# Where the normed rows are scaled: by row before the transposes or by column after them, in a three-block fp32 kernel

## The chip, the cores and the metric

One core of one Trainium2 chip. The metric is the time of one execution in microseconds (us) on the device, the median of several runs. TensorE (PE) has a granted clock that the profile shows as PEclk, 1.00 for full speed.

## The reference, cut to what matters

All tensors are fp32; 256 tokens, 1024 features, one batch. A vector `c` modulates the first two layers, and a memory of 256 rows feeds a cross-attention.

```python
c_act = silu(c)                                   # c / (1 + exp(-c)), 1024 numbers
for l in range(2):
    sh_m, sc_m, g_m, sh_f, sc_f, g_f = split(c_act @ ada_w[l] + ada_b[l], 6)
    h = modulate(rmsnorm(x, norm_g[l, 0]), sh_m, sc_m)      # h * (1 + scale) + shift, per feature
    if l == 0:  y = short_conv_mixer(h, ...)
    else:       # kv: its own shift, scale from c_act @ kv_ada_w + kv_ada_b and its own norm of the same x
                y = mla_mixer(h, ..., shared_kv(x, c_act, ...))
    x = x + g_m * rmsnorm(y, norm_g[l, 1])
    h = modulate(rmsnorm(x, norm_g[l, 2]), sh_f, sc_f)
    x = x + g_f * rmsnorm(relu(h @ mlp_up[l]) ** 2 @ mlp_down[l], norm_g[l, 3])
h = rms_norm(x, norm_mix);    x = x + concat(hgrn2(h @ w_in), moba(h @ w_in)) @ w_out
h = rms_norm(x, norm_xattn);  x = x + cross_attention(h, rms_norm(mem, norm_mem), w_q, w_k, w_v, w_o)
h = rms_norm(x, norm_mlp);    x = x + relu(h @ w_ff1) ** 2 @ w_ff2
return rms_norm(x, norm_final)
```

## The kernel before, in words

**Stages.** In this order: K and V of the memory (lines 553 to 618), the first norm (L620), conv mixer, MLP0, MLA (kv and q projections, attention, output), MLP1, HGRN and MoBA, cross-attention, MLP2, final norm. The residual x stays on chip as two token tiles `xt[tt]` of 128 tokens by 1024 features, each in halves `hf` of 512. Matmuls want features on the partitions, so each normed tile is transposed, 128x128 at a time, on PE.

**Three-term products.** Every fp32 operand is kept as a rounded part and the rest, and a product is three matmuls (`mm3`, `mm3t`, L237 to L246). `split_into` makes the parts: the high one on ScalarE (ACT, L220), the low one on VectorE (DVE, L221). Weights come by `load` (SP's DMA queue, into one of 7 raw buffers) and `split`.

**Order of work.** The program is written stage by stage, and each engine's order is then set by a scheduler from priorities (the order written; `tc.high_priority()` puts a block ahead of what waits beside it) and free buffers. Each engine then runs its own list in that order. `behind(marks, f)` issues what f issues after the marked instructions (the last high and low part that a norm wrote).

**Modulation.** `c_act @ ada_w` is done on DVE, one column of 128 outputs at a time: `ada_part`'s step loads 512 KB and multiplies it with `cb`, silu(c) on all partitions (L306, 112 steps). `background()`, called at each split, runs a planned number of such steps. `row(g)` turns 8 columns of 128 into a 1024-wide row on all partitions: two copies (gb), eight PE transposes (L326), two ACT copies. A norm before a modulated stage takes two rows, `norm_rows`: gain and shift. `to_features` then does, per half of a token tile:

```python
nc.vector.scalar_tensor_tensor(v, xt[tt][:, hf, :], r, a[:, c], op0=OP.mult, op1=OP.mult)   # L407
nc.vector.tensor_add(v, v, sh[:, c])                                                        # L409
nc.tensor.transpose(m[:, j * P:(j + 1) * P], v[:, j * P:(j + 1) * P], ident)                # L412, four
hi = activation(m, Copy); lo = m - hi                                                       # L398, L399
```

This happens at the first norm (L620 to L623), into MLP0 (m0, after conv_out), into MLA (two norms of one x: kv and q, `into_mla`), and into MLP1 (m1). The norms of the second half of the program have a gain row from DRAM and no shift.

**The opening.** `cb` is a DMA of c to all partitions, then exp, add, reciprocal and product on 128x1024 (L291 to L297). The memory's tiles are scaled by column and split (L560, L561); the K product (L237 to L239) starts with them; 16 modulation steps run beside it and x's first norm stands after the V product.

**Ends of projections.** `down` accumulates in four banks, acc[tt][hf]; its last 6 weight pieces (TAIL) are done for tt=0 first and tt=1 after, so that tt=0's norm runs beside tt=1's matmuls. `Mlp.rest` does the same. `Mlp.first`/`squares` make MLP pieces: relu, transposes, a copy (rT), square and split.

## Time and profile before

| | |
|---|---|
| Runs | 1062.53 us median of 3 (1059.4 to 1064.05) |
| Profiled execution | 1059.84 us; span 1058.0 us; mean granted PE clock 0.981 |
| Busy share of the span | PE 96% (1012.3 us, 6186 instructions), DVE 73% (768.3 us), ACT 52% (547.2 us), POOL 0% |
| DMA | 231.58 MB, mean 219 GB/s |
| Chain of work that ended last | PE 84%, DVE 8%, ACT 4%, issue 2%, DMA 1% |

The chain is followed back from the last instruction through whatever released each step, so its shares add up to the span. The busy shares are means over stages with different limits: PE fills most of the span, and what is left for any change to take is either PE work itself or the places where PE stands or runs below its full clock.

### The profile page before, as it was taken

The numbers are of one execution on the slowest core, as the hardware profiler recorded it, in microseconds if no ns is written. First come the engines' busy times: TensorE is split into PE (matmuls) and PEld (weight loads), VectorE is DVE, ScalarE is ACT, GpSimd is POOL, SyncE is SP. The second block draws the span as 40 slices with busy tenths as digits, with TensorE's granted clock in tenths as the row PEclk, the third lists the DMA queues.
The fourth block names the chain that finished last, engine by engine and source line by source line (L and its number), as shares of the span: only waits on it lengthen the run. The fifth ranks groups of instructions, "written<-read, shape, count | busy, mean of one in ns | idle before, by whom it ended". The sixth has DMA issues, their size and how long they took to land.

```text
span 1058.0 us, 16057 instructions
## 1 busy us (share of the span) xinstructions
PE 1012.3 (96%) x6186; PEld 882.9 (83%) x6186; DVE 768.3 (73%) x1140; ACT 547.2 (52%) x872; POOL 1.0 (0%) x8
## 2 busy tenths in 40 slices
PE   4989999999999979999999999999899999999997
PEld 4869997898898768677999888898678988998885
DVE  7889998998888699759765554778567557555552
ACT  5344456654345564768444444754246446544441
POOL 0000000000000000000000000000000000000000
PEclk9999999999999989999999999999799999999999
DMA  7979996899998369616876663755214426666511
GB/s 282 354 265 359 322 327 230 289 374 347 318 346 312 105 208 371 218 41 228 302 236 194 196 182 118 263 193 179 73 48 155 145 101 236 183 189 188 185 55 40
DMA packets 64876, 231.58 MB, mean 219 GB/s; under 512 B 7201, under 2 KB 7585, under 8 KB 64801
## 3 DMA queue, kind: packets, MB, share of 16 engines
q1 hardware_dynamic: 64512, 229.93, 63.2%
q8 instruction: 48, 0.79, 0.3%
q10 hardware_dynamic: 288, 0.65, 0.2%
q14 instruction: 28, 0.22, 0.1%
HBM read 229.50 MB, written 1.05 MB: 218 GB/s over the span
## 4 chain that ended last, share of the span: by engine, by line
PE 84%; DVE 8%; ACT 4%; issue 2%; DMA 1%; DVEq 0%; SPq 0%; ACTq 0%
PE u L238 11%; PE acc L246 11%; PE acc L244 11%; PE u L237 11%; PE u L239 11%; PE acc L245 11%; PE u L245 4%; PE u L246 4%; PE u L244 4%; PE m L249 3%; DVE wlo L221 2%; PE acc L249 1%; DVE raw L306 1%; ACT whi L220 1%; DMA raw<-in_w_xk_dram 1%
## 5 line engine op out<-in xcount | busy, mean ns | idle before, releaser
L221 DVE TENSOR_TENSOR wlo<-raw,whi 128x1024 fp32r<-128x1024 f32 (+1 forms) x317 | 380.1, 1212 | 138.9 <-ACT whi L220 135.9
L220 ACT ACTIVATE whi<-raw 128x1024 fp32r<-128x1024 f32 (+1 forms) x317 | 328.0, 1049 | 250.2 <-PE u L238 100.6
L238 PE MATMUL u<-hl,whi 128*128 128x256 f32 x960 | 271.2, 283 | 0.0
L239 PE MATMUL u<-hh,wlo 128*128 128x256 f32 x960 | 270.5, 282 | 0.0
L237 PE MATMUL u<-hh,whi 128*128 128x256 f32 x960 | 270.3, 282 | 0.0
L238 PEld LDWEIGHTS u<-hl,whi 128*128 128x128 f32 x960 | 181.3, 189 | 3.6 <-issue 2.5
L237 PEld LDWEIGHTS u<-hh,whi 128*128 128x128 f32 x960 | 181.8, 190 | 1.1 <-ACT hh L398 0.2
L239 PEld LDWEIGHTS u<-hh,wlo 128*128 128x128 f32 x960 | 181.5, 189 | 0.0
L244 PE MATMUL acc<-whi,mh 128*128 128x512 f32 x384 | 151.8, 395 | 0.0
L246 PE MATMUL acc<-wlo,mh 128*128 128x512 f32 x384 | 151.6, 395 | 0.0
L245 PE MATMUL acc<-whi,ml 128*128 128x512 f32 x384 | 151.4, 394 | 0.0
L306 DVE SCALAR_TENSOR_TENSOR raw<-raw,cb 128x1024 f32<-128x1024 f32 x112 | 135.7, 1219 | 11.0 <-DMA raw<-in_adaT_dram 11.0
L246 PEld LDWEIGHTS acc<-wlo,mh 128*128 128x128 f32 x384 | 72.2, 188 | 16.8
L245 PEld LDWEIGHTS acc<-whi,ml 128*128 128x128 f32 x384 | 72.2, 188 | 16.0
L244 PEld LDWEIGHTS acc<-whi,mh 128*128 128x128 f32 x384 | 72.1, 188 | 15.7
L245 PE MATMUL u<-whi,hl 128*128 128x512 f32 x144 | 57.9, 402 | 1.0 <-DVE hl L399 1.0
L244 PE MATMUL u<-whi,hh 128*128 128x512 f32 x144 | 57.1, 396 | 0.5 <-ACT hh L398 0.4
L246 PE MATMUL u<-wlo,hh 128*128 128x512 f32 x144 | 57.2, 397 | 0.0
L353 ACT ACTIVATE sq<-x 128x512 f32<-128x512 f32 x32 | 20.0, 627 | 43.6 <-DVE x L381 34.0
L470 ACT ACTIVATE rl<-u 128x512 f32<-128x512 f32 x36 | 21.1, 586 | 28.7 <-PE u L239 28.5
L437 DVE TENSOR_TENSOR ml<-rq,mh 128x512 fp32r<-128x512 f32 x48 | 33.1, 690 | 3.4 <-ACT mh L435 0.2
L436 DVE TENSOR_TENSOR rq<-rl 128x512 f32<-128x512 f32 x36 | 24.7, 687 | 13.6 <-ACT rl L470 13.6
(281 smaller groups left out, 1292.7 us busy)
## 6 DMA issues: line engine op xcount, KB each, us to landing
raw<-in_adaT_dram SPq DMA_DIRECT2D x112, 512.0 KB, 5.3
raw<-in_mlp_up_w_dram SPq DMA_DIRECT2D x64, 512.0 KB, 5.0
raw<-in_mlp_down_w_dram SPq DMA_DIRECT2D x64, 512.0 KB, 4.5
raw<-in_w_ff_dram SPq DMA_DIRECT2D x64, 512.0 KB, 3.6
raw<-in_w_in_dram SPq DMA_DIRECT2D x28, 512.0 KB, 4.0
raw<-in_conv_in_w_dram SPq DMA_DIRECT2D x24, 512.0 KB, 5.4
raw<-in_w_xk_dram SPq DMA_DIRECT2D x8, 512.0 KB, 6.4
raw<-in_w_xv_dram SPq DMA_DIRECT2D x8, 512.0 KB, 6.3
```

What stands on the lines that cost most here:

```text
L220: nc.scalar.activation(hi, view, AF.Copy)
L221: nc.vector.tensor_sub(lo, view, f32(hi))
L237: nc.tensor.matmul(o, wh, xh, start=start, stop=False, skip_group_check=True)
L238: nc.tensor.matmul(o, wh, xl, start=False, stop=False, skip_group_check=True)
L239: nc.tensor.matmul(o, wl, xh, start=False, stop=stop, skip_group_check=True)
L244: nc.tensor.matmul(o, xh, wh, start=start, stop=False, skip_group_check=True)
L245: nc.tensor.matmul(o, xl, wh, start=False, stop=False, skip_group_check=True)
L246: nc.tensor.matmul(o, xh, wl, start=False, stop=stop, skip_group_check=True)
L249: nc.tensor.matmul(o, a, b, start=start, stop=stop, skip_group_check=True)
L306: nc.vector.scalar_tensor_tensor(raw, raw, 1.0, cb, op0=OP.mult, op1=OP.mult, accum_out=mods[:, base + j:base + j + 1])
L436: nc.vector.tensor_mul(q, h_, h_)
L437: nc.vector.tensor_sub(lo, q, f32(hi))
```

## The change

- **silu(c)** is taken on 8 columns of 128 (`cact`, 128x8) and `row(cact)` spreads it: eight transposes in place of the DMA of cb and of the four 128x1024 operations. The transposes' identity is loaded first on SP's queue.
- **The memory's operand** is scaled by ACT into `memg` and split with 512-wide operations, two features' tiles at once.
- **The first norm**: x is loaded, normed and transposed within the K product (`first_x`); the modulation steps are ordered so that four of them give two feature tiles of gain and shift, and `first_h` builds those two tiles of h (per-column scale and shift on ACT, then the split). The rows are gone.
- **`modulated`** takes the place of `norm_rows` and `to_features` into m0, MLA and m1: x times rstd, transposes, then gain and shift per feature column with the features on the partitions, four 128x128 operations for each half, then high and low part. Into MLA x is transposed once for both norms, kv being scaled on ACT, q on DVE. No gain or shift row is made any more; `row` no longer makes gb copies.
- **`tail`**: tt=0's last pieces are done bank by bank (hf 0, then hf 1); for the last MLP tt=1's too (`by_half`). `final` multiplies by the gain before rstd is known and shares the last scaling between DVE and ACT.
- **`norm_done()`** holds later splits and modulation steps behind the last norm's high part (on ACT) and low part (on DVE).
- The evacuations of `up`, `squares` and of the kv and q units stand under `high_priority`; tt=1's units use accumulator banks; `squares` multiplies before the transposes, so the rT copy is gone.

Counts in the program, before and after: PE matmuls 5989 and 5901 (gain and shift rows' transposes 112 and 32, eight new for silu, x's transposes 128 and 112), ACT 792 and 835, DVE 1022 and 990; SP's transfers 450 both.

```diff
+        with ExitStack() as st_:
+            for ins in norm_end:
+                st_.enter_context(tc.issue_after(ins))
+            split_into(hi[:, :n], lo[:, :n], raw)
...
-                evac(n // 2, u)
+                with tc.high_priority():
+                    evac(n // 2, u)
...
+    def tail(parts, accs, last, by_half=False):
+
+        for hf in range(2):
+            for w, x, k in parts:
+                down_step(w, x, accs, (0,), k == 0, k == last, (hf,))
+        for hfs in ((0,), (1,)) if by_half else ((0, 1),):
+            for w, x, k in parts:
+                down_step(w, x, accs, (1,), k == 0, k == last, hfs)
...
+    def row(g):
+
+        r = big("row", D)
+        for hf in range(2):
+            m = mtile()
+            for j in range(4):
+                k = 4 * hf + j
+                nc.tensor.transpose(m[:, j * P:(j + 1) * P], g[:, k:k + 1].to_broadcast([P, P]), ident)
+            nc.scalar.activation(r[:, hf * 512:hf * 512 + 512], m, AF.Copy)
+        return r
...
-    cb = big("cb", D)
-    nc.scalar.dma_start(cb, t["c"][None, :].to_broadcast([P, D]))
-    ce = big("ce", D)
-    nc.scalar.activation(ce, cb, AF.Exp, scale=-1.0)
-    nc.vector.tensor_scalar(ce, ce, 1.0, None, op0=OP.add)
-    nc.vector.reciprocal(ce, ce)
-    nc.vector.tensor_mul(cb, cb, ce)
+    marks = {}
+    norm_end = []
+
+    def norm_done():
+
+        norm_end[:] = [marks["act"], marks["dve"]]
+
+    cact = col("cact", 8)
+    nc.scalar.activation(cact, vcol("c", 0, 8), AF.Exp, scale=-1.0)
+    nc.vector.tensor_scalar(cact, cact, 1.0, None, op0=OP.add)
+    nc.vector.reciprocal(cact, cact)
+    nc.vector.tensor_mul(cact, cact, vcol("c", 0, 8))
+    nc.sync.dma_start(ident, t["consts"][:, :128])
+    cb = row(cact)
...
+    def ada_step(n):
+        raw = load(t["adaT"][n])
+        with ExitStack() as st_:
+            for ins in norm_end[1:]:
+                st_.enter_context(tc.issue_after(ins))
+            nc.vector.scalar_tensor_tensor(raw, raw, 1.0, cb, op0=OP.mult, op1=OP.mult, accum_out=mods[:, n:n + 1])
...
-    def norm_rows(l, scale, shift, g):
-
-        c = col("gn", 8)
-        nc.vector.scalar_tensor_tensor(c, mod(l, scale), 1.0, g, op0=OP.add, op1=OP.mult)
-        return row(c), row(mod(l, shift))
+    def gain(l, part, g):
+        a = col("gn", 8)
+        nc.vector.scalar_tensor_tensor(a, mod(l, part), 1.0, g, op0=OP.add, op1=OP.mult)
+        return a
...
-    def to_features(tt, r, rows, h, one=False):
-
...
+    def to_features(tt, a, h):
+
+        r = x_rstd(tt)
...
             v = tmp("xs", 512)
-            nc.vector.scalar_tensor_tensor(v, xt[tt][:, hf, :], r, a[:, c], op0=OP.mult, op1=OP.mult)
-            if sh is not None:
-                nc.vector.tensor_add(v, v, sh[:, c])
+            nc.vector.scalar_tensor_tensor(v, xt[tt][:, hf, :], r, a[:, hf * 512:hf * 512 + 512],
+                                           op0=OP.mult, op1=OP.mult)
+            m = mtile()
+            for j in range(4):
+                nc.tensor.transpose(m[:, j * P:(j + 1) * P], v[:, j * P:(j + 1) * P], ident)
+            split_features(m, h.ks(0, 4 * hf, 4, tok(tt)), h.ks(1, 4 * hf, 4, tok(tt)))
+
+    def modulated(tt, sets, one=False):
+
+        r = x_rstd(tt)
+        for hf in range(2):
+            v = tmp("xs", 512)
+            nc.vector.tensor_scalar(v, xt[tt][:, hf, :], r, None, op0=OP.mult)
...
-            split_features(m, h.ks(0, 4 * hf, 4, sl), h.ks(1, 4 * hf, 4, sl))
+            if len(sets) > 1:
+                v = tmp("xf", 512)
+                nc.scalar.activation(v, m, AF.Copy)
+                m = v
+            for i, (a, sh, h) in enumerate(sets):
+                g = tmp("h32", 4, P)
+                for j in range(4):
+                    k = 4 * hf + j
+                    x = m[:, j * P:(j + 1) * P]
+                    if i:
+                        nc.vector.tensor_scalar(g[:, j, :], x, a[:, k:k + 1], sh[:, k:k + 1], op0=OP.mult, op1=OP.add)
+                    else:
+                        nc.scalar.activation(g[:, j, :], x, AF.Identity, scale=a[:, k:k + 1], bias=sh[:, k:k + 1])
+                hi = h.ks(0, 4 * hf, 4, sl)
+                marks["act"] = nc.scalar.activation(hi, g, AF.Copy).ins
+                marks["dve"] = nc.vector.tensor_sub(h.ks(1, 4 * hf, 4, sl), g, f32(hi)).ins
...
-        for tt in range(2):
-            for k in range(n0, n):
-                down_step(ws[k - n0], x(k), accs, (tt,), k == 0, k == n - 1)
+        tail([(ws[k - n0], x(k), k) for k in range(n0, n)], accs, n - 1)
...
+            with tc.high_priority():
+                self.squares(u, tt, b)
+
...
+            q = tmp("rq", 512)
+            nc.vector.tensor_mul(q, r, r)
...
-                nc.tensor.transpose(m[:, j * P:(j + 1) * P], r[:, j * P:(j + 1) * P], ident)
-            rT = tmp("rT", 4, P)
-            nc.scalar.activation(rT, shaped(m, [4, P]), AF.Copy)
+                nc.tensor.transpose(m[:, j * P:(j + 1) * P], q[:, j * P:(j + 1) * P], ident)
             hi, lo = self.mid(b)
-            squared(rT, hi[:, :, tok(tt)], lo[:, :, tok(tt)])
...
+            split_into(hi[:, :, tok(tt)], lo[:, :, tok(tt)], shaped(m, [4, P]))
...
+        vg = tmp("memg", 2, S)
         for j in range(2):
-            k = 2 * i + j
-            nc.scalar.activation(hm.k(0, k), v[:, j, :], AF.Copy, scale=gm[:, k:k + 1])
-            nc.vector.scalar_tensor_tensor(hm.k(1, k), v[:, j, :], gm[:, k:k + 1], f32(hm.k(0, k)),
-                                           op0=OP.mult, op1=OP.subtract)
+            nc.scalar.activation(vg[:, j, :], v[:, j, :], AF.Copy, scale=gm[:, 2 * i + j:2 * i + j + 1])
+        split_into(hm.ks(0, 2 * i, 2), hm.ks(1, 2 * i, 2), vg)
...
+    ga, gb1 = col("ga", 8), col("gb1", 8)
+    nc.vector.scalar_tensor_tensor(gb1, vcol("ada_b", 8, 8), 1.0, norm_g(0, 0), op0=OP.add, op1=OP.mult)
...
+    def first_h(j):
+        sl = slice(j, j + 2)
+        nc.vector.tensor_mul(ga[:, sl], mods[:, 8 + j:10 + j], norm_g(0, 0)[:, sl])
+        nc.vector.tensor_add(ga[:, sl], ga[:, sl], gb1[:, sl])
+        nc.vector.tensor_add(mods[:, sl], mods[:, sl], vcol("ada_b", j, 2))
+        v = tmp("h32", 2, S)
+        for i in range(2):
+            k = j + i
+            nc.scalar.activation(v[:, i, :], xn[k // 4][:, k % 4, :], AF.Identity, scale=ga[:, k:k + 1],
+                                 bias=mods[:, k:k + 1])
+        split_into(h.ks(0, j, 2), h.ks(1, j, 2), v)
...
+    def first_x(tt):
+        r = x_rstd(tt)
+        for hf in range(2):
+            v = tmp("xs", 512)
+            nc.scalar.activation(v, xt[tt][:, hf, :], AF.Copy, scale=r)
+            m = mtile()
+            for j in range(4):
+                nc.tensor.transpose(m[:, j * P:(j + 1) * P], v[:, j * P:(j + 1) * P], ident)
+            nc.scalar.activation(xn[hf][:, :, tok(tt)], shaped(m, [4, P]), AF.Copy)
+
+    for j in range(0, KT, 2):
+        for n in (8 + j, j, 9 + j, j + 1):
+            steps.append(((0, 0), lambda n=n: ada_step(n)))
+        steps.append(((0, 0), lambda j=j: first_h(j)))
+    pace["rate"] = len(steps) / MEM_PIECES
...
-    h = H("h")
-    rows = norm_rows(0, 1, 0, norm_g(0, 0))
-    for tt in range(2):
-        to_features(tt, xr[tt], rows, h)
+    flush((0, 0))
...
-            u = utile()
+            u = atile(0) if tt else utile()
...
+                modulated(tt, [mla["kv"] + (hkv,), mla["q"] + (hq_,)], one=True)
...
-        mla["kv"] = norm_rows("kv", 1, 0, vcol("kv_norm_g", 0, 8))
-        mla["q"] = norm_rows(1, 1, 0, norm_g(1, 0))
+        mla["kv"] = gain("kv", 1, vcol("kv_norm_g", 0, 8)), mod("kv", 0)
+        mla["q"] = gain(1, 1, norm_g(1, 0)), mod(1, 0)
...
+            with tc.high_priority():
+                ss = col("ss", 2)
+                for hf in range(2):
+                    v = xt[tt][:, hf, :]
+                    nc.vector.tensor_add(v, v, accs[tt][hf])
+                    nc.scalar.activation(tmp("sq", 512), v, AF.Square, accum_out=ss[:, hf:hf + 1])
+                    nc.vector.tensor_mul(v, v, gfr[:, hf * 512:hf * 512 + 512])
+                r = rstd(ss, D)
+                for hf in range(2):
+                    v = xt[tt][:, hf, :]
+                    if hf:
+                        nc.scalar.activation(v, v, AF.Copy, scale=r)
+                    else:
+                        nc.vector.tensor_scalar(v, v, r, None, op0=OP.mult)
+                    nc.sync.dma_start(out[tt * P:(tt + 1) * P, hf * 512:hf * 512 + 512], v)
...
+    m2.rest(h, final, by_half=True)
```

**Opening, DVE** (ce and cb: the chain of silu on 1024 columns; cact: the new one; hml: the low part of the memory's operand; wlo: of a weight). Before:

```order
L221 TENSOR_TENSOR wlo<-raw,whi 128x1024
L295 TENSOR_SCALAR ce<-ce 128x1024
L561 SCALAR_TENSOR_TENSOR hml<-memT,vec,hmh 128x256
L296 RECIPROCAL ce<-ce 128x1024
L561 SCALAR_TENSOR_TENSOR hml<-memT,vec,hmh 128x256
L297 TENSOR_TENSOR cb<-cb,ce 128x1024
L561 SCALAR_TENSOR_TENSOR hml<-memT,vec,hmh 128x256 x2
L221 TENSOR_TENSOR wlo<-raw,whi 128x1024
```

After:

```order
L324 TENSOR_SCALAR cact<-cact 128x8
L920 TENSOR_TENSOR lm<-vec,lm 128x4
L921 TENSOR_TENSOR lm<-vec,lm 128x4
L325 RECIPROCAL cact<-cact 128x8
L326 TENSOR_TENSOR cact<-cact,vec 128x8
L221 TENSOR_TENSOR wlo<-raw,whi 128x1024
L221 TENSOR_TENSOR hml<-memg,hmh 128x512
L221 TENSOR_TENSOR wlo<-raw,whi 128x1024
```

The three 128x1024 operations that stood between the first low parts are gone; five small ones stand ahead of them.

**From conv_out into MLP0, ACT** (sq: sums of squares of tt=1's accumulators; hh: high parts; h_1782 and h_1796: tt=0's two halves). Before:

```order
L353 ACTIVATE sq,ss<-x 128x512 x2
L363 ACTIVATE rstd<-ss,sb 128x1
L364 ACTIVATE rstd<-rstd 128x1
L353 ACTIVATE sq,ss<-acc_1635 128x512
L353 ACTIVATE sq,ss<-acc_1636 128x512
L398 ACTIVATE hh<-m 128x4x128 x2
```

After:

```order
L456 ACTIVATE h_1782<-m,mods,gn 128x128 x4
L456 ACTIVATE h_1796<-m,mods,gn 128x128
L376 ACTIVATE sq,ss<-acc_1603 128x512
L376 ACTIVATE sq,ss<-acc_1604 128x512
L458 ACTIVATE hh<-h_1782 128x4x128
L456 ACTIVATE h_1796<-m,mods,gn 128x128 x2
L386 ACTIVATE rstd<-ss,sb 128x1
L456 ACTIVATE h_1796<-m,mods,gn 128x128
L387 ACTIVATE rstd<-rstd 128x1
L458 ACTIVATE hh<-h_1796 128x4x128
```

In both, tt=0's high parts stand behind the squares of tt=1's accumulators; five of the eight new scalings stand ahead of those squares and three behind.

**Into MLA, ACT** (hkvh, hqh: high parts of the kv and q operands; xf: the shared transposed x). Before:

```order
L398 ACTIVATE hkvh<-m 128x512 x2
L353 ACTIVATE sq,ss<-acc_2082 128x512
L353 ACTIVATE sq,ss<-acc_2083 128x512
L363 ACTIVATE rstd<-ss,sb 128x1
L364 ACTIVATE rstd<-rstd 128x1
L398 ACTIVATE hqh<-m 128x512
L353 ACTIVATE sq,ss<-x 128x512 x2
L398 ACTIVATE hqh<-m 128x512
```

After:

```order
L446 ACTIVATE xf<-m 128x512
L456 ACTIVATE h_3651<-xf,mods,gn 128x128 x4
L458 ACTIVATE hkvh<-h_3651 128x512
L446 ACTIVATE xf<-m 128x512
L458 ACTIVATE hqh<-h_3658 128x512
L456 ACTIVATE h_3674<-xf,mods,gn 128x128
L376 ACTIVATE sq,ss<-acc_2058 128x512
L376 ACTIVATE sq,ss<-acc_2059 128x512
L456 ACTIVATE h_3674<-xf,mods,gn 128x128 x3
L386 ACTIVATE rstd<-ss,sb 128x1
L458 ACTIVATE hkvh<-h_3674 128x512
```

kv's second half, which stood ahead of the squares of tt=1's accumulators, now stands behind them; q's first half stands ahead.

## Rows read from the trace of the kernel before

**Rows 1.** Busy time by stretch: us, engines' busy us (instructions), PEclk, DMA share, GB/s.
```profile
0.00:20.00 20.00, 6.26 (x26) 5.68 (x27) 12.83 (x18) 13.72 (x21) 0.48 (x7) 0.92 0.83 314
20.00:40.00 20.00, 17.49 (x129) 17.09 (x129) 18.81 (x26) 7.27 (x10) 0.00 (x0) 0.90 0.81 270
60.00:80.00 20.00, 15.54 (x76) 12.48 (x75) 16.48 (x29) 9.50 (x14) 0.00 (x0) 0.88 0.61 233
120.00:140.00 20.00, 20.00 (x171) 20.00 (x171) 20.00 (x32) 10.11 (x13) 0.00 (x0) 1.00 0.92 301
170.00:190.00 20.00, 18.98 (x90) 14.96 (x90) 18.69 (x27) 12.66 (x27) 0.00 (x0) 1.00 0.47 158
364.85:395.57 30.72, 23.58 (x131) 20.94 (x129) 28.95 (x46) 20.10 (x50) 0.00 (x0) 0.89 0.49 167
400.00:420.00 20.00, 20.00 (x138) 17.71 (x137) 19.30 (x42) 7.28 (x13) 0.00 (x0) 1.00 1.01 384
```

**Rows 2.** PE's longest wait in the opening by releaser: total us, times, longest.
```profile
PE u L237 <- ACT hmh L560: 9.8, 1, 9.8
```

**Rows 3.** Timeline, opening: start us, us, operation, [idle before <- releaser].
```profile
10.55 6.55 DVE L296 RECIPROCAL ce<-ce 128x1024 f32<-128x1024 f32 x1
17.46 0.58 PE L238 MATMUL u<-hml,whi 128*128 128x256 f32 x1 [3.84 <-DVE hml L561]
...
33.12 0.39 PE L237 MATMUL u<-hmh,whi 128*128 128x256 f32 x1 [2.51 <-DVE memK L600]
...
72.48 1.26 PE L412 MATMUL m<-ident,xs 128*128 128x128 f32 x8 [1.51 <-DVE xs L409]
...
76.29 1.94 PE L412 MATMUL m<-ident,xs 128*128 128x128 f32 x8 [2.56 <-DVE xs L409]
...
78.06 0.79 PE L237 MATMUL u<-hh,whi 128*128 128x256 f32 x2
```

**Rows 4.** PE's timeline, gain and shift rows near the end of MLP0.
```profile
342.04 1.03 PE L326 MATMUL m<-ident,gb 128*128 128x128 f32 x8
342.83 0.48 PE L244 MATMUL acc<-whi,mh 128*128 128x512 f32 x1
343.33 1.15 PE L326 MATMUL m<-ident,gb 128*128 128x128 f32 x8
344.24 0.48 PE L245 MATMUL acc<-whi,ml 128*128 128x512 f32 x1
```

**Rows 5.** Instructions of one line: ns least/median/most, from start to start.
```profile
L407 DVE SCALAR_TENSOR_TENSOR xs<-x,rstd,row x32: 742/746/753, 69.8 to 873.0; 128x512 f32<-128x512 f32 x32
L409 DVE TENSOR_TENSOR xs<-xs,row x20: 682/684/695, 71.7 to 486.0; 128x512 f32<-128x512 f32 x20
L943 DVE TENSOR_SCALAR hk<-hk x2: 402/402/402, 711.6 to 713.1; 128x512 f32<-128x512 f32 x2
L529 DVE TENSOR_SCALAR pexp<-pexp,sml x16: 277/348/355, 778.8 to 843.6; 128x256 f32<-128x256 f32 x12, 128x128 f32<-128x128 f32 x4
L1036 ACT ACTIVATE ot<-ot,oss x8: 387/392/401, 760.7 to 779.3; 128x128 f32<-128x128 f32 x8
L699 ACT ACTIVATE kx<-m x2: 261/269/277, 386.9 to 395.0; 128x128 f32<-128x128 f32 x2
L398 ACT ACTIVATE hh<-m x24: 589/598/601, 73.2 to 874.7; 128x512 fp32r<-128x512 f32 x24
```

**Rows 6.** Timelines around m0 (ACT, at 174 us) and MLA (PE).
```profile
172.78 0.60 ACT L353 ACTIVATE sq<-acc 128x512 f32<-128x512 f32 x1 [2.74 <-PE acc L246]
...
174.06 1.08 ACT L398 ACTIVATE hh<-m 128x512 fp32r<-128x512 f32 x2
...
371.67 0.45 PE L244 MATMUL u<-whi,hqh 128*128 128x384 f32 x1 [1.60 <-ACT whi L220]
```

**Rows 7.** Timeline of the end, DVE and SP's queue.
```profile
1053.49 1.41 DVE L1133 SCALAR_TENSOR_TENSOR x<-x,rstd,row 128x512 f32<-128x512 f32 x2 [1.10 <-ACT rstd L364]
...
1054.27 0.99 SPq L1134 DMA_DIRECT2D out_dram<-x  x2
```

More of the change, by code (lines that the diff above doesn't have):

```diff
@@ L316, in mod @@
         return mods[:, base:base + 8]
-    def row(g):
-        r = big("row", D)
-        for hf in range(2):
-            gb = tmp("gb", 4, P)
-            nc.vector.tensor_copy(gb, g[:, 4 * hf:4 * hf + 4, None].to_broadcast([P, 4, P]))
-            m = mtile()
-            for j in range(4):
-                nc.tensor.transpose(m[:, j * P:(j + 1) * P], gb[:, j, :], ident)
-            nc.scalar.activation(r[:, hf * 512:hf * 512 + 512], m, AF.Copy)
-        return r
     def gate_row(l, part, i):
@@ L486, in rest, with into_mlp @@
             ws = [piece(self.wd[k], D) for k in range(n0, 4 * nb)]
-            for tt in range(2):
-                for k in range(n0, 4 * nb):
-                    down_step(ws[k - n0], x(k), accs, (tt,), False, k == 4 * nb - 1)
+            tail([(ws[k - n0], x(k), k) for k in range(n0, 4 * nb)], accs, 4 * nb - 1, by_half)
             finish(accs)
             pace["hold"] = False
-    def into_mlp(m, update, rows):
+    def into_mlp(m, update, norm):
         h = H("h")
@@ L500, in chain @@
                     update(tt, accs[tt])
-                    to_features(tt, x_rstd(tt), rows, h)
+                    norm(tt, h)
             chain(0)
@@ L573, in net @@
                 nc.vector.tensor_add(sqs, sqs, q)
-        if i == 0:
-            nc.sync.dma_start(ident, t["consts"][:, :128])
     us = [utile() for _ in range(2)]
@@ L705, in q_unit @@
                 mm3t(u[:, :384], (w[0][:, k % 2, :], w[1][:, k % 2, :]), hk(hq_, k, slice(0, P)), k == 0, k == KT - 1)
-            r = rstd(one_sum(u[:, :384]), 384)
-            c = tmp("ql", 384)
-            nc.vector.scalar_tensor_tensor(c, u[:, :384], r, lat[:, 256:640], op0=OP.mult, op1=OP.mult)
-            m = mtile()
-            for j in range(3):
-                nc.tensor.transpose(m[:, j * P:(j + 1) * P], c[:, j * P:(j + 1) * P], ident)
-            split_features(m, mla["qc"][0][:, :, tok(tt)], mla["qc"][1][:, :, tok(tt)], 3)
+            with tc.high_priority():
+                r = rstd(one_sum(u[:, :384]), 384)
+                c = tmp("ql", 384)
+                nc.vector.scalar_tensor_tensor(c, u[:, :384], r, lat[:, 256:640], op0=OP.mult, op1=OP.mult)
+                m = mtile()
+                for j in range(3):
+                    nc.tensor.transpose(m[:, j * P:(j + 1) * P], c[:, j * P:(j + 1) * P], ident)
+                split_features(m, mla["qc"][0][:, :, tok(tt)], mla["qc"][1][:, :, tok(tt)], 3)
         hs = []
@@ L1120, in net @@
     m2 = Mlp(t["w_ff1_2"], t["w_ff2_2"])
-    h, fin = into_mlp(m2, add, fixed_rows(2))
+    nmr = fixed_rows(2)
+    h, fin = into_mlp(m2, add, lambda tt, h_: to_features(tt, nmr, h_))
     down(t["w_xo_2"], lambda k: hk(o, k), 8, fin)
-    gfr, _ = fixed_rows(3)
+    gfr = fixed_rows(3)
     def final(accs):
         for tt in range(2):
-            add(tt, accs[tt])
-            r = x_rstd(tt)
-            for hf in range(2):
-                v = xt[tt][:, hf, :]
-                nc.vector.scalar_tensor_tensor(v, v, r, gfr[:, hf * 512:hf * 512 + 512], op0=OP.mult, op1=OP.mult)
-                nc.sync.dma_start(out[tt * P:(tt + 1) * P, hf * 512:hf * 512 + 512], v)
-    m2.rest(h, final)
+            with tc.high_priority():
+                ss = col("ss", 2)
[13 more added lines that the diff above has]
+    m2.rest(h, final, by_half=True)
 NBIG, NRAW, NW, NTMP = 21, 7, 9, 7
```

70 lines of the change are left out of this document (34 added, 36 removed).

## The prediction, before the run

> **What bounds the kernel now.** I read the busy table first: PE is busy 96% of the span, so only two things can be taken away: PE's own work, or the places where PE stands or runs below full clock. The busy time by stretch [rows 1] shows where those are. Between 120 and 140 us PE is busy 20.00 of 20 us, and so it is at 400 to 420: nothing to win there except matmuls. Three kinds of stretch are different. The opening has 6.26 of 20 us and 17.49 of 20, at a granted clock of 0.92 and 0.90, and 15.54 at 0.88 around 70 us. The way into MLA, 364.85 to 395.57, has 23.58 of 30.72 us at 0.89, while DVE is busy 28.95 there: DVE is its bound. The ends are short. Next I read PE's waits [rows 2] and the timeline of the opening [rows 3], where each row names the releaser. PE's first matmul waits until 9.8 us for the memory's high part; then 3.84 us for a low part, because DVE runs a reciprocal of 6.55 us ahead of it; 2.51 us for a memK evacuation; and 1.51 and 2.56 us for the first norm's halves. The conv mixer starts at 78.06 us.
>
> **The sum is made against the profiled execution, 1059.84 us**, 2.7 under the median of the runs shown, 1062.53; I subtract the gain from the median for the forecast. About 0.5%, 5.3 us, is what a measurement of this kernel can tell from no change.
>
> **Opening.** The wide exp, add, reciprocal and product and the copy of c go; the rows of the first norm go; so do its two products and adds on DVE. To come off PE's path: the four idle stretches, 3.84 + 2.51 + 1.51 + 2.56 = 10.4 us [rows 3]; 16 transposes of the rows, which cost 0.117 us each where such rows are seen apart (342.04 to 342.83 and 343.33 to 344.24, 16 of them in 0.79 + 0.91 us [rows 4], plus about 0.09 for each restart: 0.94 for eight): 1.9 us; and the clock, 6.26 x 0.08 + 17.49 x 0.10 + 15.54 x 0.12 = 4.1 us [rows 1]. That is 16.4 at most. Least is the wait behind the reciprocal alone, 3.84. I keep waits of 5.4 us in it: 2.51 for the memK evacuation, which the change hardly touches, and 2.9 for the new chain (silu's row, then four modulation steps, then two tiles of h), about what one of the old norm waits was. So **11 us**. Two checks. DVE must lose as much, since it is busy 18.81 of 20 us there: 6.55 for the reciprocal and 4 x 0.746 + 4 x 0.684 for the norm [rows 3, 5] are 12.3. The transfers must fit: 78 us of work in 67 raise a share of 0.83 to 0.97; 1.01 is seen at 400 us [rows 1].
>
> **The rows for kv and q.** Their four rows are 32 transposes in the middle of full PE work. Four times 0.94 is **3.7 us** [rows 4], with little doubt; the gb copies and row copies beside them on DVE and ACT were hidden.
>
> **Into MLA.** DVE loses 8 x 0.746 + 8 x 0.684 = 11.4 us. It gains four products with rstd, 402 ns by the nearest 512-wide one, and 16 scalings of q; their nearest rows run from 277 ns (128 wide) [rows 5]: 1.6 + 4.4 = 6.0. DVE would let the stretch be 5.4 shorter. ACT gets four copies and 16 scalings of kv: 4 x 0.598 + 16 x 0.392 = 8.7 us on top of 20.10. If none of its other work moves, ACT needs 28.8 of the 30.72, a gain of 2. Part of that other work is weight splits, which the change queues behind the norms anyway, so I stay nearer to DVE's limit: **4 us**. The bounds are 0 (a wait like the 1.60 us at 371.67 for a weight's high part [rows 6] grows, as the splits stand later now) and 7.1, all the idle time there. The eight transposes per token tile that are saved lie inside this stretch and are not counted again.
>
> **Into MLP0 and MLP1.** Each loses two rows, 16 transposes or 1.9 us; 3.7 together. Against that, a half of h was one ACT operation of 598 ns and is now four more before it. An ACT scaling of 128 columns takes 392 ns, or 269 read from an accumulator bank [rows 5]: 1.1 to 1.6 us in the chain for each half. Some of it stands ahead of the accumulators' end, with tt=1's matmuls as cover; if that cover is gone, all of it shows. I charge 1.7 for both places and take **2 us**, with 0 and 3.7 as bounds. The Trainium skill speaks against this part ("VectorE: DVE Perf Modes", section "The TRN2 errata — SBUF-src ops pay a fixed extra latency per instruction"): each ScalarE or VectorE instruction carries a fixed cost, and tiles of 512 or more are advised. By its cycle table a 128-wide ScalarE operation would be 0.25 to 0.29 us, an estimate from that page; the trace agrees in kind, with 0.392 for 128 columns against 0.598 for 512, and is dearer. With the page's figures this term would be about 2.3 (1.7 less a fifth, from 3.7).
>
> **The end.** The last token tile's first scaling may share its time with ACT: one of two scalings of about 0.7 us (1.41 for two [rows 7]) goes, and the square and rstd stay in series. **0.6 us**; between 0 and 1.4.
>
> **At nothing:** the half-by-half tails (the same matmuls; conv_out's needs six pieces in half the time, under 1 us if a split is late); the evacuations under high priority, the rT copy and the transposed squares (ACT and DVE have room in the full PE stretches); ident first on SP's queue (PE's first matmul waits on ACT's hmh, not on it). Queuing modulation steps and splits behind norms delays filler on ACT and DVE; what would be late next is a weight's parts, the 1.60 us case above. POOL and SP lose nothing and get nothing; the 512 KB of cb leaves ACT's queue.
>
> **Sum:** 11 + 3.7 + 4 + 2 + 0.6 = 21.3. From 1059.84 that is 1038.5; from the median, **1041**.
>
> **Rivals.**
> *More* (0.15): the new chain in the opening never stalls PE, MLA loses all its idle time, and the ACT chain is covered: 16.4 + 3.7 + 7.1 + 3.7 + 0.6 = 31.5, 1031. For it: DVE was the releaser in nearly all of these waits, and it loses the most work. Against: ACT takes it over.
> *Less* (0.20): only the reciprocal's wait goes in the opening, because DVE is then full with splits and modulation steps and the conv stage (20.00 of 20 us on DVE at 120 to 140, share of DMA 0.92 [rows 1]) has no room to take any of them; MLA is bound by ACT and gains 1; the norms gain nothing: 3.8 + 3.7 + 1 + 0.6 = 9.1, 1053.
> *Slower* (0.05): ACT runs its list in order. Into m0, tt=0's high parts already stand behind the squares of tt=1's accumulators: after waiting 2.74 us for PE, the squares run at 172.78 and the parts only at 174.06 [rows 6]. Now up to three more operations per half stand there, in m0, m1 and MLA (kv's second half has moved behind them). PE then has nothing to run, and its clock falls as it has in MLA (0.89). The price of such a place is what MLA loses today: 7.1 idle and 23.58 x 0.11 = 2.6 of clock, 9.7 [rows 1]. Three are 29.1, against 19.0 that the other parts give (11 + 3.7 + 3.7 + 0.6): 10 slower, 1073. It decides from 6.3 us in each place. Against it: in m0 the squares wait for matmuls that have to run anyway, and PE is idle for only 1.0 us of the 20 from 170 us, at full clock [rows 1]. The Trainium skill ("TensorE: Matmul & The Clock Gate", in the table ahead of "What a matmul computes") lists ScalarE and VectorE queues as strictly first in, first out; the trace agrees, as the high parts above stand behind the squares.
> *No change* (0.05): the change doesn't do what it says where it matters: silu is short, but the steps that need `cb` come no earlier, because the transfers come no faster, and the norm's waits become waits for ACT in equal size. Then only part of the 3.7 for the kv and q rows is left: 1059 to 1062.
>
> **How the numbers follow.** The forecast has 0.55. Faster takes the forecast, more and less: 0.55 + 0.15 + 0.20 = 0.90; within 0.5%: 0.05; slower: 0.05. The range: opening 3.84 to 16.4, MLA 0 to 7.1, norms 0 to 3.7 don't fall to their ends together; to 1030 and to 1054 it takes in more and less, and leaves out no change and slower, 0.10, and about as much of tails in the other cases.
>
> **What would show it.** Conv starts at about 67 us in place of 78.06; no wait of 3.84 for a low part; PE's clock in the first three stretches above 0.90; no L326 rows in MLP0 beyond the gates; the way into MLA some 27 us long with DVE below 26 busy. Wrong: new PE waits on ACT (h or high parts) of over 2 us at m0, MLA or m1; a fall of the clock in places that had 1.00; a wait for splits queued behind norms. If conv starts at 67 and the total still gains under 10, the conv stage gave it back.

## The result, and the profile after

The changed kernel takes 1049.64 us (median of four runs, 1047.0 to 1050.67) against 1061.1 beside it: a ratio of 0.9885, 95% interval 0.9853 to 0.9917. Run again beside other kernels it took 1050.23, ratio 0.9906 (0.9883 to 0.9929). So it is faster, by about 10 to 12 us where 21 were forecast. Ratios are of fast runs; one run of all those told here, of 5535.54 us in the first experiment, is left out as slow. Its line numbers are new: L309 transposes a row, L335 is a modulation step, L376 the squares, L456 the scalings by column, L458 the high part of h, L728 the conv mixer's cg, L240 to L242 and L247 to L249 the three-term matmuls.

Busy time by stretch, columns as in [rows 1], the last row being the way into MLA; then 140 to 160 us of the kernel before:

```profile
0.00:20.00 20.00, 13.53 (x79) 12.64 (x80) 12.41 (x23) 15.94 (x27) 0.48 (x7) 1.00 0.92 343
20.00:40.00 20.00, 20.00 (x161) 19.45 (x160) 14.72 (x29) 15.46 (x32) 0.00 (x0) 1.00 0.90 345
60.00:80.00 20.00, 16.54 (x110) 15.32 (x110) 15.21 (x25) 8.72 (x12) 0.00 (x0) 0.91 0.91 331
120.00:140.00 20.00, 17.86 (x153) 17.66 (x151) 20.00 (x32) 7.38 (x11) 0.00 (x0) 1.00 0.96 335
140.00:160.00 20.00, 18.97 (x70) 15.17 (x71) 13.36 (x17) 11.76 (x16) 0.00 (x0) 0.83 0.92 346
355.70:383.06 27.36, 19.66 (x115) 17.01 (x113) 23.79 (x46) 24.61 (x66) 0.00 (x0) 0.99 0.47 152
```

```profile
140.00:160.00 20.00, 19.87 (x133) 17.66 (x132) 19.61 (x31) 12.95 (x17) 0.00 (x0) 1.00 0.93 331
```

The opening is as it should be: 13.53 us of PE work in the first 20 us where there were 6.26, and a full second stretch. But 120 to 140 us was full and is not, and the stretch after it, where the clock had been full, has 0.83. PE's largest waits (total us, times, longest) name the reason:

```profile
PE u L247 <- ACT hh L458: 4.3, 2, 2.5
PE m L309 <- DVE cact L326: 4.1, 1, 4.1
PE acc L247 <- ACT whi L220: 3.2, 1, 3.2
...
PE u L240 <- ACT whi L220: 2.7, 1, 2.7
PE acc L247 <- ACT pexp L568: 1.9, 2, 1.4
PE u L240 <- ACT hmh L220: 1.9, 1, 1.9
...
PE u L247 <- ACT whi L220: 1.7, 1, 1.7
```

Most of them name ACT. PE's timeline, where these waits stand and where the steps of the prediction can be read:

```profile
66.19 0.39 PE L240 MATMUL u<-hh,whi 128*128 128x256 f32 x1 [2.70 <-ACT whi L220]
...
141.03 0.79 PE L247 MATMUL acc<-whi,zh 128*128 128x512 f32 x1 [3.17 <-ACT whi L220]
...
169.07 0.49 PE L247 MATMUL u<-whi,hh 128*128 128x512 f32 x1 [1.77 <-ACT hh L458]
...
359.30 0.41 PE L247 MATMUL u<-whi,hkvh 128*128 128x320 f32 x1 [1.66 <-ACT hkvh L458]
...
383.06 0.79 PE L240 MATMUL u<-ck,whi 128*128 128x256 f32 x2 [0.47 <-ACT ck L419]
...
466.26 0.50 PE L247 MATMUL u<-whi,hh 128*128 128x512 f32 x1 [2.48 <-ACT hh L458]
```

The same places in three profiles (us from the span's start to the first matmul of the stage; "ahead" is before less changed):

| first matmul of | before | changed | ahead | changed, again | ahead |
|---|---|---|---|---|---|
| K of the memory | 9.78 | 7.95 | 1.83 | 9.51 | 0.27 |
| conv mixer | 78.06 | 66.19 | 11.87 | 67.50 | 10.56 |
| conv_out | 148.84 | 141.03 | 7.81 | 142.34 | 6.50 |
| MLP0, token-major | 174.70 | 169.07 | 5.63 | 167.63 | 7.07 |
| MLP0, first accumulation | 212.60 | 207.72 | 4.88 | 206.27 | 6.33 |
| MLA (kv) | 364.85 | 355.70 | 9.15 | 354.26 | 10.59 |
| K from kv | 395.57 | 383.06 | 12.51 | 382.64 | 12.93 |
| MLA's output | 434.09 | 422.03 | 12.06 | 421.56 | 12.53 |
| MLP1, token-major | 475.19 | 466.26 | 8.93 | 462.70 | 12.49 |
| w_out | 771.45 | 758.95 | 12.50 | 757.65 | 13.80 |
| last matmul | 1051.03 | 1038.50 | 12.53 | 1037.78 | 13.25 |

The conv mixer starts as much earlier as was forecast, and the start of conv_out takes 4.06 us of it back, in both profiles. In the three places with a norm in front (MLP0, MLA, MLP1) the rows' transposes went and a wait for ACT came.

### The profile page after: what moved, and what is told of

Read it like the earlier page. It is cut to its first block, busy times and chain, and to the rows that moved or that the text cites. A ratio compares the mean times of both kernels' runs of the same rounds, so it can differ in the third digit from the quotient of the medians.

```text
span 1045.2 us, 15837 instructions
## 1 busy us (share of the span) xinstructions
PE 1003.4 (96%) x6098; PEld 873.7 (84%) x6098; DVE 736.0 (70%) x1108; ACT 560.7 (54%) x916; POOL 1.0 (0%) x8
## 4 chain that ended last, share of the span: by engine, by line
PE 87%; DVE 6%; ACT 4%; issue 1%; DMA 1%; SPq 0%; ACTq 0%
PE acc L247 11%; PE acc L249 11%; PE acc L248 11%; PE u L241 11%; PE u L240 11%; PE u L242 11%; PE u L249 4%; PE u L248 4%; PE u L247 4%; PE m L252 3%; DVE wlo L221 2%; DVE raw L335 2%; PE acc L252 2%; ACT h L456 1%; PE u L252 1%
## 5 line engine op out<-in xcount | busy, mean ns | idle before, releaser
L240 PE MATMUL u<-hh,whi 128*128 128x256 f32 x960 | 270.7, 282 | 2.7 <-ACT whi L220 2.7
L242 PE MATMUL u<-hh,wlo 128*128 128x256 f32 x960 | 271.2, 283 | 0.8 <-DVE wlo L221 0.8
L240 PEld LDWEIGHTS u<-hh,whi 128*128 128x128 f32 x960 | 182.2, 190 | 4.0 <-ACT whi L220 3.1
L242 PEld LDWEIGHTS u<-hh,wlo 128*128 128x128 f32 x960 | 181.8, 189 | 1.1 <-DVE wlo L221 1.0
L247 PE MATMUL acc<-whi,mh 128*128 128x512 f32 x384 | 151.7, 395 | 0.0
L249 PE MATMUL acc<-wlo,mh 128*128 128x512 f32 x384 | 151.6, 395 | 0.0
L335 DVE SCALAR_TENSOR_TENSOR raw<-raw,row 128x1024 f32<-128x1024 f32 x112 | 135.9, 1220 | 5.4 <-DMA raw<-in_adaT_dram 5.4
L249 PEld LDWEIGHTS acc<-wlo,mh 128*128 128x128 f32 x384 | 72.3, 188 | 16.7
L247 PEld LDWEIGHTS acc<-whi,mh 128*128 128x128 f32 x384 | 72.2, 188 | 15.8
L247 PE MATMUL u<-whi,hh 128*128 128x512 f32 x144 | 58.8, 409 | 4.3 <-ACT hh L458 4.3
L249 PE MATMUL u<-wlo,hh 128*128 128x512 f32 x144 | 58.5, 406 | 0.0
L247 PEld LDWEIGHTS u<-whi,hh 128*128 128x128 f32 x144 | 27.9, 194 | 11.1 <-ACT hh L458 4.9
L248 PEld LDWEIGHTS u<-whi,hl 128*128 128x128 f32 x144 | 27.9, 194 | 7.3 <-DVE hl L459 1.4
```

The costliest lines, as they stand in the source:

```text
L240: nc.tensor.matmul(o, wh, xh, start=start, stop=False, skip_group_check=True)
L242: nc.tensor.matmul(o, wl, xh, start=False, stop=stop, skip_group_check=True)
L247: nc.tensor.matmul(o, xh, wh, start=start, stop=False, skip_group_check=True)
L248: nc.tensor.matmul(o, xl, wh, start=False, stop=False, skip_group_check=True)
L249: nc.tensor.matmul(o, xh, wl, start=False, stop=stop, skip_group_check=True)
L335: nc.vector.scalar_tensor_tensor(raw, raw, 1.0, cb, op0=OP.mult, op1=OP.mult, accum_out=mods[:, n:n + 1])
```

## The experiments

**What makes PE wait at the norms?** Theory A: the narrow scalings on ACT. First, rows again at MLP0 and MLP1:

```diff
-        a, sh = gain(0, 4, norm_g(0, 2)), mod(0, 3)
+        a, sh = row(gain(0, 4, norm_g(0, 2))), row(mod(0, 3))
...
-        h, fin = into_mlp(m0, ..., lambda tt, h_, a=a, sh=sh: modulated(tt, [(a, sh, h_)]))
+        h, fin = into_mlp(m0, ..., lambda tt, h_, a=a, sh=sh: by_rows(tt, (a, sh), h_))
```

> The changed kernel (profiled at 1047.0 us) with the norms into MLP0 and MLP1 done by rows again (two rows each, products and shift on VectorE, one wide high part on ScalarE). Theory A: the changed kernel loses there because four narrow scalings stand in ScalarE's list ahead of each high part, so TensorE waits (1.77 and 2.48 us before the first matmuls) and then runs at half clock. Then the two waits shrink to about 0.4 us, some 3 us of slow matmuls go, and 3.7 us of row transposes come back: 6.5 - 3.7, about 3 us faster, 1044. Rival B: the half-by-half tails make the waits; then they stay and the transposes are added: 3 to 4 us slower, 1050 to 1051.

Ratio to before 0.9913 (0.9883 to 0.9943), not faster than the changed kernel. The waits did shrink (into MLP0 to 0.22 us for a low part, into MLP1 to 0.69), but the 3.7 us of transposes came back with them: from conv_out to MLP0 and from MLA's output to MLP1 it is 66.30 us together, and 66.43 in the changed kernel run again. So B's waits did not stay, and A is wrong on the sum. On the cause A is not shown either, as the edit also moves high parts: into MLP0 hh now runs between the two squares of tt=1's accumulators. Then the scalings shared between two engines:

```diff
-                    if i:
+                    if i or (len(sets) == 1 and j % 2):
```

> The changed kernel with two of the four scalings of a half done on VectorE instead of ScalarE at MLP0 and MLP1. Theory A: the chain on ScalarE ahead of each high part is about 0.8 us shorter per half, the waits of 1.77 and 2.48 us fall to about 1, and with them part of the slow matmuls: 2 to 4 us faster, 1043 to 1045. Rival B (tails) and rival D (the two squares of tt=1's accumulators in the middle of the chain, not the scalings): within 1 us of 1047.

0.9909 (0.9879 to 0.994); the waits are 1.68 and 2.38 us, for 1.78 and 2.49. The chain did not become 0.8 us shorter, because the two engines took turns. ACT and DVE (L454 is its scaling) into MLP0:

```profile
168.13 0.46 ACT L456 ACTIVATE h<-m,mods,gn 128x128 f32<-128x128 f32 x1 [1.52 <-PE m L442]
169.07 0.81 ACT L456 ACTIVATE h<-m,mods,gn 128x128 f32<-128x128 f32 x2 [0.48 <-DVE h L454]
169.77 0.59 ACT L376 ACTIVATE sq<-acc 128x512 f32<-128x512 f32 x1
```

```profile
168.62 0.41 DVE L454 TENSOR_SCALAR h<-m,gn,mods 128x128 f32<-128x128 f32 x1 [1.09 <-ACT h L456]
169.56 0.76 DVE L454 TENSOR_SCALAR h<-m,gn,mods 128x128 f32<-128x128 f32 x2 [0.53 <-ACT h L456]
```

From the first scaling to the first square it is 1.64 us, and 1.73 in the changed kernel run again (164.05 to 165.78). So this run does not decide between the scalings (A) and the squares (D); the last experiment below does in part.

**The tails**, tt=0 whole again:

```diff
-        for hf in range(2):
-            for w, x, k in parts:
-                down_step(w, x, accs, (0,), k == 0, k == last, (hf,))
+        for w, x, k in parts:
+            down_step(w, x, accs, (0,), k == 0, k == last)
```

> The changed kernel with tt=0's last six pieces done both halves at a time, as before the change (the last MLP's tt=1 still by halves). Theory A (ScalarE's narrow scalings make the waits at the norms): first half of tt=0's norm starts no earlier, so within 1.5 us of 1047. Rival B (the tails by halves starve something: six pieces are wanted in half the time, and the waits for weights' parts follow): 3 to 6 us faster, 1041 to 1044.

0.9884 (0.9835 to 0.9933), waits of 2.01 and 2.49 us. B falls by the waits, which stay; the total of four runs, with 5 us to either side, could hardly tell B's 3 us from none.

**The evacuations**, without `tc.high_priority()` around `evac(n // 2, u)`:

> The changed kernel without high priority for the evacuations of the feature-major projections (conv, MLP up, HGRN and MoBA, cross-attention q). In the traces the HGRN and MoBA stage is 3.3 us shorter after the change, which nothing I costed explains. Theory C: the evacuations under priority shorten it; then it is 3 to 4 us longer here, 1050 to 1051. Rival: the stage's gain came from where the slow clock fell, or from VectorE's and ScalarE's other order; then within 1 us of 1047 here.

0.9886 (0.9828 to 0.9944). From HGRN's first product of hv and kT to w_out it takes 22.3 us here and in the changed kernel run again, against 18.7 in its first profile and 21.7 before: the 3 us were an accident of one execution. C falls, and the slow clock of its rival is what differs. The first row is the changed kernel's first profile, the second its run again; PE's busy time differs by the whole 3.7 us, at a granted clock of 0.82 and 0.65:

```profile
740.28:758.95 18.67, 15.81 (x143) 11.40 (x142) 10.51 (x43) 4.93 (x15) 0.00 (x0) 0.82 0.14 49
735.31:757.65 22.34, 19.54 (x143) 14.26 (x142) 11.03 (x46) 4.94 (x15) 0.00 (x0) 0.65 0.10 37
```

**conv_out's first piece.** ACT's timeline in the changed kernel, 133 to 144 us, and DVE's from 136 us:

```profile
134.08 1.06 ACT L310 ACTIVATE row<-m 128x512 f32<-128x512 f32 x2
139.40 0.63 ACT L220 ACTIVATE zh<-cg 128x512 fp32r<-128x512 f32 x1 [4.26 <-DVE cg L728]
139.94 3.88 ACT L220 ACTIVATE whi<-raw 128x1024 fp32r<-128x1024 f32 x4
```

```profile
136.38 1.23 DVE L335 SCALAR_TENSOR_TENSOR raw<-raw,row 128x1024 f32<-128x1024 f32 x1
...
137.53 1.23 DVE L335 SCALAR_TENSOR_TENSOR raw<-raw,row 128x1024 f32<-128x1024 f32 x1
...
138.67 0.69 DVE L728 TENSOR_TENSOR cg<-cg,u 128x512 f32<-128x512 f32 x1
```

PE is done at 137.86 (141.03 less its wait). ACT stands still for 4.26 us with the weight's high part (whi) next but one in its list: the last zh is ahead of it and waits for cg, which needs PE's last unit and so could not start before 137.86. From there PE's 3.17 us are 0.81 for a modulation step ahead of cg on DVE, 0.73 for cg, 0.54 for zh and 1.09 for whi. PE wants this whi at once and the last zh only for the last two pieces. The piece's transfer was issued at 131.80 and landed 5.8 us later, at 137.6, so whi stood ready for 2.3 us; by the order of the list that is what PE could have been spared of the 3.17, an estimate from these rows. The Trainium skill ("TensorE: Matmul & The Clock Gate", the table ahead of "What a matmul computes") calls this queue strictly first in, first out; the trace agrees, as whi runs at 139.94, behind zh. Three edits put pieces earlier:

```diff
+            if n == 2 and at:
+                at()
...
+               at=(lambda: early.append(piece(t["conv_out_w"][0], D))) if i == 5 else None)
```

> The changed kernel with one move: conv_out's first weight piece is loaded and split ahead of the conv mixer's last two pieces, so that its high part stands ahead of the last zh in ScalarE's list. Theory E: the change lost 4.1 us in the conv stage because that high part stood behind zh, which waits for VectorE's cg, itself among modulation steps; TensorE waited 3.16 us in every profile so far and mostly ran slow matmuls for some 5 us after. Then the wait goes and about 2 us of slow matmuls with it: 4 to 5 us faster than the changed kernel, 1045. Rival F: VectorE or the transfers are the bound there, and the next piece is late instead: within 1 us of 1049.6.

0.9878 (0.9859 to 0.9898), 1047.44 us. The wait became 1.49 us at the second piece, and the wait into MLP0 2.72. Against the changed kernel's two ratios (0.9885 and 0.9906) that is 0.7 to 3 us, within the intervals: less than E said, and it does not tell F from E.

> The same, and the conv mixer's first weight piece split under high priority ahead of the V product's last unit (its ScalarE operation then stands ahead of the last tiles of h). Theory E: of the 2.70 us that TensorE waits for it at the start of the conv mixer about 1 goes: 1 us faster than the run with conv_out's piece alone, 1044. Rival F: the last h tile is then what TensorE waits for, no difference.

0.9886 (0.9866 to 0.9906). The wait at conv's start fell from 2.70 to 1.72 us and 1.89 us for a low part came at conv_out: nothing gained.

> The changed kernel with conv_out's first two weight pieces loaded and split ahead of the conv mixer's last two pieces. With one piece early the wait of 3.16 us became 1.49 us at the second piece. Theory E: with two no wait over 0.5 us is left before conv_out's tail and the kernel is 4 to 5 us faster than the changed one beside it. Rival F: VectorE (full in the conv stage) makes the third piece or a low part late instead, or the MLP's first high part waits longer, as it did (2.72 for 1.77 us): 1 to 3 us faster.

0.9885 (0.986 to 0.991). No wait is left at conv_out, and the one into MLP0 is 3.18 us. ACT there:

```profile
163.88 1.85 ACT L458 ACTIVATE h<-m,mods,gn 128x128 f32<-128x128 f32 x5 [1.27 <-PE m L444]
165.61 0.61 ACT L378 ACTIVATE sq<-acc 128x512 f32<-128x512 f32 x1
...
166.18 0.62 ACT L378 ACTIVATE sq<-acc 128x512 f32<-128x512 f32 x1
...
166.75 0.66 ACT L460 ACTIVATE hh<-h 128x512 fp32r<-128x512 f32 x1
```

hh runs at 166.75, in the changed kernel beside it at 166.92. PE gained 3 us and handed them to the next wait. tt=0's accumulators were ready no earlier (its first squares run at 155.77, in the other at 155.68), and its chain from there to hh is 11 us long; only tt=1's matmuls, which had hidden it, ended 3 us sooner. E falls as to the gain; what F named as late next was right for MLP0.

**The queuing**, with `norm_done()` empty:

> The changed kernel without the queuing of splits and modulation steps behind the norms. If the queuing works as it is meant, weights' high parts now slip between the norm's operations on ScalarE and each of the norms into MLP0, MLA and MLP1 is 1 to 2 us later: 3 to 6 us slower, 1053 to 1056. Rival: the scheduler's order hardly changes, as the norms stand under high priority anyway: within 1 us of 1049.6.

0.991 (0.9888 to 0.9932); the way into MLA is 29.53 us, for 27.36 and 28.38. It may be worth 1 to 2 us there; the total does not tell it from nothing, nor the rival from the theory.

**The opening in two halves.** The kernel before with silu on 8 columns alone (cact, its transposes, ident first):

> The kernel before with silu on 8 columns alone (row by transposes, identity loaded first), everything else as before. If the reciprocal's wait was the opening's worth of it, the 3.84 us wait for a low part and some slow matmuls go: 4 to 5 us faster than before, ratio 0.996. If the opening is bound by VectorE as a whole, the 8.5 us of wide operations go and later waits (2.51 for memK, 1.51 and 2.56 at the norm) shrink too: 7 to 9 us faster, 0.992. If transfers bound it: under 2 us.

0.9953 (0.9935 to 0.9971). Conv starts at 70.83 us and conv_out at 141.57: 7.2 us ahead of before at the first, 7.3 at the second. So silu alone gives 7 of the opening's 10.6 us and loses none of it up to there, and at conv_out it is ahead of the whole change run again (142.34). By the starts and by the profiles (1052.83 against 1059.84) that is the second of the three expectations, by the ratio, 5 us, nearer the first; of the later waits memK's fell to 1.39 us and the last at the norm stayed at 2.56. Next the changed kernel again, as a reference:

> The changed kernel as it is, as a reference beside the next two. Its first profile was ahead of its siblings in two places that none of their edits touches (1.5 to 2 us at the first matmul, 3 us between HGRN and the output projection). If these are accidents of one execution, the profile here shows a span near 1049 and the stage from HGRN to the output projection at about 21.6 us, not 18.7; if they belong to the kernel, 1045 again.

1050.23 us; HGRN to w_out 22.3, K's first matmul at 9.51. So both were accidents of one execution. The span in the profile is 1044.5 all the same and not 1049, as the profiled run was the fastest of the six (1046.32); profiles lie up to 4 us under the median here.

And, beside it, the whole change without the tile-by-tile operand (the first norm by rows after the V product):

> The changed kernel with the opening's first norm as it was (gain and shift rows after the modulation steps, x's norm after the V product), silu and all else as changed. Silu alone brought the conv mixer's start to 70.8 us, the whole change to 67.8. Theory G: the three us that the tile-by-tile operand gives are lost again, as it moves conv_out's first weight split behind the last zh in ScalarE's list (3.16 us of waiting and the slow matmuls after it). Then conv starts at about 71, conv_out waits under 0.5 us, and the total is within 1.5 us of the changed kernel, 1048 to 1051. Rival: the 3.16 us come from the other parts (priorities, tails), then they stay and the total is about 3 us slower, 1053.

**1044.45 us**, ratio 0.9866 (0.9842 to 0.989), against 1050.23 and 0.9906 (0.9883 to 0.9929) for the changed kernel beside it; five of its six runs are under the fastest of the changed kernel's six. Conv starts 4.4 us later (71.94), conv_out at 141.91 without a wait, MLP0 at 165.23, 2.4 us earlier. ACT at conv_out and into MLP0:

```profile
138.27 1.99 ACT L220 ACTIVATE whi<-raw 128x1024 fp32r<-128x1024 f32 x2
141.75 0.60 ACT L310 ACTIVATE row<-m 128x512 f32<-128x512 f32 x1 [1.49 <-PE m L309]
142.36 0.63 ACT L220 ACTIVATE zh<-cg 128x512 fp32r<-128x512 f32 x1
...
162.66 1.86 ACT L469 ACTIVATE h<-m,mods,gn 128x128 f32<-128x128 f32 x5 [1.66 <-PE m L455]
164.39 0.65 ACT L471 ACTIVATE hh<-h 128x512 fp32r<-128x512 f32 x1
164.91 0.61 ACT L376 ACTIVATE sq<-acc 128x512 f32<-128x512 f32 x1
```

Two pieces stand ahead of the last zh, and hh ahead of the squares. G's mechanism holds; no difference in total, as it forecast, is too little: the tile-by-tile operand costs more than it gives. By the profiles the conv stage takes 69.97 us for 74.84, which makes up for the later start, and from conv_out to MLP0 it is 23.32 for 25.29. Last, both ideas together: the first norm by columns but whole, and the squares of tt=1's accumulators behind tt=0's last high part:

```diff
-        ss = sums(acc)
+        ss = behind([marks["act"]], lambda: sums(acc)) if tt else sums(acc)
```

> Two edits on the run with the first norm by rows (1044.45 us). The first norm is done by columns like the others, whole and after the V product; and the squares of tt=1's accumulators are queued behind tt=0's last high part into MLP0, MLA and MLP1. Theory H: what TensorE waits for at these places is not the narrow scalings (sharing them with VectorE left 1.68 of 1.77 us) but the high part's place behind the two squares of tt=1's accumulators, some 1.3 to 2 us of ScalarE and their own wait for TensorE; where the scheduler put the first high part ahead of them, into MLP0 in the run with the first norm by rows, the wait was gone. Then the 2.48 us into MLP1 fall to about 1 and the 1.66 us into MLA to about 1, with some slow matmuls: 2 to 4 us; the opening loses 16 row transposes and the wait for the shift row, 2 to 3 us. Together 1039 to 1042. Rival J: tt=1's norm, later by its squares, is then what TensorE waits for, and the gain is given back one unit later: 1043 to 1046.

1046.21 us, 0.9865 (0.9835 to 0.9896), level with the run before. ACT into MLP1, where the changed kernel had two squares between h and hh:

```profile
464.25 1.85 ACT L469 ACTIVATE h<-m,mods,gn 128x128 f32<-128x128 f32 x5 [1.27 <-PE m L455]
465.98 0.64 ACT L471 ACTIVATE hh<-h 128x512 fp32r<-128x512 f32 x1
...
468.24 0.58 ACT L376 ACTIVATE sq<-acc 128x512 f32<-128x512 f32 x1
```

H's argument from the shared scalings does not hold (above), but PE's waits fell as it says: into MLP1 from 2.49 to 1.32 us, into MLA from 1.67 to 0.50; J's show up too (0.51 and 0.67 us for tt=1 into MLP0, 0.46 and 0.65 into MLP1, x's transposes in MLA 1.97 for 0.74). The conv mixer starts 60.95 us after K's first matmul (71.09 less 10.14), by rows 63.25 (71.94 less 8.69): 2.3 us gained, as forecast. Shown is that the squares' place makes 1.17 us of the wait in each of the two places, with the scalings unchanged; what makes the other 1.32 into MLP1, the scalings among it, was not taken apart. That moving the squares pays is not shown.

## Why the prediction was right in sign and half right in size

- **The opening, 11 us.** Right where it is read: conv starts 10.6 to 11.9 us earlier, no 3.84 us for a low part (0.43 now), the clock 1.00 in the first two stretches. Silu alone is 7 of it. From K's first matmul to conv's, before, changed and changed again (columns as in [rows 1]):

```profile
9.78:78.06 68.28, 57.36 (x332) 50.90 (x332) 60.69 (x86) 32.86 (x55) 0.00 (x0) 0.93 0.83 308
7.95:66.19 58.24, 52.94 (x316) 46.51 (x316) 46.51 (x81) 39.45 (x70) 0.00 (x0) 1.00 0.93 350
9.51:67.50 57.99, 52.54 (x316) 46.12 (x316) 46.49 (x81) 39.34 (x70) 0.00 (x0) 1.00 0.91 345
```

  PE's idle time falls by 5.6 and 5.5 us (5.0 forecast: 10.4 less 5.4) and its work and clock together by 4.4 and 4.8 (6.0 forecast); the rest, 1.8 and 0.3, is K's earlier start. The waits that stay, 5.3 us, are as long as those the prediction kept, but others: memK's is gone, and 1.7 and 2.7 us are for weights' high parts on ACT. To that extent the 11 is luck.
- **The step that failed** is taking those 11 us to the end of the span, with the split of weights "at nothing". The conv stage is 4.06 us longer (74.84 for 70.78), 3.17 of it one wait for a weight's high part. The rival "less" had the stage, but as lack of room on DVE; it is ACT's list, in which a ready operation stood behind one that waited for PE's last unit and then for DVE. The prediction looked at what each engine has to do, and at ACT's order only at the norms.
- **Rows for kv and q, 3.7.** From MLP0's first accumulation to MLA the change gains 4.27 and 4.26 us. Right.
- **Into MLA, 4.** 3.36 and 2.34 us, between the bounds given, but not by the mechanism forecast. DVE fell from 28.95 to 23.79 us as reckoned, and PE's idle time did not fall with it: 7.14 us before, 7.70 and 7.05 after. What fell is PE's busy time, by 3.92 and 2.25 us, with 16 to 17 instructions fewer, the transposes that the prediction did not count for themselves, and in the first profile a clock of 0.99 for 0.89. The number is luck. ACT rose from 20.10 to 24.61 us, and PE now waits for it (1.66 us for hkvh) as for DVE. In the changed kernel run again:

```profile
354.26:382.64 28.38, 21.33 (x114) 18.71 (x112) 23.92 (x46) 24.67 (x67) 0.00 (x0) 0.89 0.44 154
```

- **Into MLP0 and MLP1, 2.** From conv_out's start to MLP0's: 25.86 us before, 28.04 and 25.29 after; from MLA's output to MLP1: 41.10, 44.23 and 41.14. Without the slow matmuls of the first profile that is 0.5, not 2: 1.9 us of transposes went in each place, and 1.4 and 2.5 us of waiting came. The rival "slower" had this mechanism, ACT's order with high parts behind the squares; its 9.7 us for each place were several times too dear, and it never came near the 6.3 from which it would have decided.
- **The end, 0.6.** From the last matmul to the end 6.97 before, 6.70 and 6.72 after: 0.3. The gain's product is done in place, and so waits for the square that reads the same tile; the last scaling on ACT (L1219) then waits 0.26 us for the product:

```profile
1038.93 0.69 DVE L1212 TENSOR_TENSOR x<-x,acc 128x512 f32<-128x512 f32 x1 [1.93 <-PE acc L249]
1040.41 0.69 DVE L1214 TENSOR_TENSOR x<-x,row 128x512 f32<-128x512 f32 x1 [0.79 <-ACT sq L1213]
1041.02 0.48 DVE L1221 TENSOR_SCALAR x<-x,rstd 128x512 f32<-128x512 f32 x1
```

```profile
1041.20 0.72 ACT L1219 ACTIVATE x<-x,rstd 128x512 f32<-128x512 f32 x1 [0.26 <-DVE x L1214]
```

- **At nothing:** right for the tails and the evacuations; the queuing is within noise.
- **The sum.** Profile against profile the gain is 12.8 (1047.0) and 13.5 us (1046.32), forecast 21.3: 4.1 went in the conv stage, 1.5 at the norms, 0.6 to 1.7 in MLA, 0.3 at the end. By medians it is 9.5 to 11.5, since both profiles of the changed kernel lie 3 to 4 us under its median. That is nearer to the rival "less" (9.1) than to the forecast, though by another mechanism than its own. Of the signs named for being wrong two showed: 2.48 us of waiting for hh into MLP1, and, in the first profile only, the clock of 0.83 where it had been 1.00.

What stays open: why the scheduler puts conv_out's first split behind the last zh in the one order and ahead in the other (only the orders and their prices were seen), and how much of the last run's two edits would stay with more runs.
